# The last head's keys rotated at once on VectorE, and a new table of durations for the attention's list scheduler

## The chip, the core and the metric

The kernel runs on one core of one Trainium2 chip. The metric is the device time of one execution in microseconds (us), as a median of several runs; lower is better. The engines are named as in the profile: PE is TensorE, DVE is VectorE, ACT is ScalarE, POOL is GpSimd, and SP issues most of the DMAs. Each engine works through its own queue in order.

## What is computed

One layer of an encoder on 1024 tokens of width 1024, in float32. Cut to what matters here:

```python
h = x @ w_in
q, k, v, z = split(h)                      # 4 heads of differential attention: 8 q/k maps of 64
q = apply_rope(q, cos, sin) * 64 ** -0.5   # t * cos + rotate_half(t) * sin
k = apply_rope(k, cos, sin)
p = softmax(where(k_chunk <= q_chunk, q @ k.T, -inf))    # block-causal, chunks of 64
a = p[:, :, 0] - lam * p[:, :, 1]          # two maps of a head are subtracted
oa = rms_norm(a @ v, subln_g)
ob = spatial_gating(gelu(z))               # the other half of the width
x = layer_norm(alpha * x + concat(oa, ob) @ w_out)
x = layer_norm(alpha * x + gated_mlp_with_conv(x))
```

## The kernel before

All large products are made of three single-pass matmuls on split operands (`mm3`: high times high, high times low, low times high), so PE has three matmuls for each tile of a product. The kernel is one stream of stages: input projections and the gating half (up to about 187 us of the span), projections of q and k with their rotation (to about 231 us), attention (to about 362 us), output projection and first layer norm (to about 440 us), gated MLP (to about 865 us) and its output projection.

**Rotation.** For head `h`, `sel` 0 (queries) or 1 (keys) and each `half` of 512 tokens, `mm3` fills one PSUM tile `pt`, and `rope_unit` gives a list of steps. `take`: ACT copies `pt` to the SBUF tile `t1`. `rotate`: SP issues four DMAs that write the rows of `t1`, swapped in blocks of 32, to `t2`. `turn`: `t1` times cos (L444, 128x512), and `t2` times sin (L444). `join`: their sum (L447). `high`: ACT makes two 64x512 high parts (L460 and L461 for queries, L463 and L465 for keys; for keys each is also copied to the other partitions by a DMA). `low`: the two 64x512 differences (L475). `turn`, `join` and `low` can run on DVE or POOL. All units run at once on DVE, but for the key units' lows, which go to POOL, and for the two units of the last head's keys. For those two, ACT copies `pt` to a tile `kr` (L502), and the steps are kept in `late`.

**Attention.** Block `n` is one head and 128 queries (`blocks`: 32 in the order of `PAIRS`). Its steps are `scores` (L545, L546, L549 on PE, for both maps), `rowmax` (L558 for more than 512 keys, one for each map; L560 for both maps at once otherwise; DVE, tile `mx`), `expo` (L570 on ACT, tile `p`), `ratio` (L584, L586, DVE, tile `nr`), `combine` (L591, DVE, writes `p`), `transp` (L608, PE), `evac` (L615, ACT or DVE), `attend` (L622, PE) and, for each pair of blocks, a norm (`norm_o` L632, `norm_mul` L656 on POOL or DVE, L674 and others). Three double PSUM tiles (`SCB = 3`) hold scores; a tile comes free when both of its exponentials are done. Beside that run `wo_load` and `wo_lo` (the first half of `w_out`, L777 on ACT, L781 on DVE or POOL), `ob_split` (L788, L789 on POOL, tile `obT`) and `fill` (parts of the output projection on PE that need no attention, added to `xn` at L811).

The order of all these is set while the program is built, by `ListScheduler`: each operation has engines, a duration (`cost`), dependences, a `rank` and resources that it takes or gives (`sc`, `p0`, `t`, `fk` and so on). At each step the operation of lowest rank that could start, by the given durations, is written into the program. What comes out is a fixed order for each engine. The ranks (`RK`, `FW`, `FO` and the others) are constants at the top. The last head's scores wait, in the scheduler, for both late key units (`need`).

Of the kernel before, what the change touches and what calls it, by code (L numbers as in the profile page):

```python
# [23 lines left out]
H = 4  # L24
# [10 lines left out]
SPAN = []  # L35
SCB = 3
WARM = 10
LATE = 151.7
FW = 112.1
FO = 59.8  # L40
FS = 53.1
# [1 line left out]
FA = 754.9  # L43
FT = -0.3
# [94 lines left out]
def hybrid_layer_kernel(  # L139
# [271 lines left out]
    def tslot(name):  # L411
        return qp.tile([P, 512], F32, tag="t", name=nm(name))
# [14 lines left out]
    def rope_unit(h, sel, half, pt):  # L427

        cols = slice(half * 512, (half + 1) * 512)
        t = {}  # L430

        def take():
            t[1] = tslot("t1")
            A.activation(t[1], pt, AF.Copy, scale=1.0 if sel else QSCALE)

        def rotate():

            t.setdefault(1, pt)
            t[2] = tslot("t2")
            for b in range(0, P, 32):  # L440
                nc.sync.dma_start(t[2][b : b + 32], t[1][b ^ 32 : (b ^ 32) + 32])

        def turn(n, eng=V):
            eng.tensor_tensor(t[n], t[n], (cos_s, sin_s)[n - 1][:, cols], op=ALU.mult)  # L444

        def join(n, eng=V):
            eng.tensor_tensor(t[1], t[1], t[2], op=ALU.add)  # L447

        def high():
            r = t[1]  # L450
            if half == 0 and sel == 0:
                stacks.append([None] * 6)
            st = stacks[h]
            names = ((0, "qs0_"), (1, "qs1_")) if sel == 0 else ((2, "kh0_"), (3, "kh1_"), (4, "kl0_"), (5, "kl1_"))
            if st[names[0][0]] is None:
                for n, name in names:
                    st[n] = stack(name)
            q0, q1, k0, k1 = st[:4]
            if sel == 0:
                A.copy(q0[LOW, cols], r[LOW])  # L460
                A.copy(q1[HIGH, cols], r[HIGH])  # L461
            else:
                A.copy(k0[LOW, cols], r[LOW])  # L463
                nc.sync.dma_start(k0[HIGH, cols].bitcast(F32), k0[LOW, cols].bitcast(F32))
                A.copy(k1[HIGH, cols], r[HIGH])  # L465
                nc.sync.dma_start(k1[LOW, cols].bitcast(F32), k1[HIGH, cols].bitcast(F32))

        def low(n, eng=V):
            r = t[1]
            q0, q1, k0, k1, l0, l1 = stacks[h]  # L470
            o, rows, hi = ((q0[HIGH, cols], LOW, q0), (q1[LOW, cols], HIGH, q1)) [n] if sel == 0 else (
                (l0[LOW, cols], LOW, k0), (l1[HIGH, cols], HIGH, k1)
            )[n]
            hi = hi[rows, cols].bitcast(F32)
            eng.tensor_tensor(o, r[rows], hi, op=ALU.subtract)  # L475
            if sel:
                other = (l0[HIGH, cols], l1[LOW, cols])[n]
                nc.sync.dma_start(other.bitcast(F32), o.bitcast(F32))

        def pick(fn, n):  # L480
            return lambda e="DVE": fn(n, V if e == "DVE" else GP)

        both, cost = ["POOL", "DVE"], {"DVE": 0.61, "POOL": 1.23}
        whole = h == H - 1 and sel == 1
        steps = [] if whole else [(["ACT"], 0.63, take)]
        steps += [(["SP"], 2.4, rotate)] + [(both, cost, pick(turn, n)) for n in (1, 2)]
        steps += [(both, cost, pick(join, 0)), (["ACT"], 1.3, high)]
        return steps + [(both, cost, pick(low, n)) for n in range(2)]

    late = []  # L490
    for h in range(H):
        wt = qw0 if h == 0 else [load_qw(h), load_qw(H + h)]
        for sel in range(2):
            for half in range(2):
                cols = slice(half * 512, (half + 1) * 512)
                pt = ps1()
                for k in range(NK):
                    w = wt[sel]
                    mm3(pt, (w[:, 0, k], w[:, 1, k]), tuple(a[:, cols] for a in xt[k]), k == 0, k == NK - 1)
                if h == H - 1 and sel == 1:  # L500
                    kr = tslot("kr")
                    A.copy(kr, pt)  # L502
                    late.append(rope_unit(h, sel, half, kr))
                else:
                    for n, (engines, _, fn) in enumerate(rope_unit(h, sel, half, pt)):
                        fn("POOL" if sel == 1 and n > 5 else "DVE") if len(engines) > 1 else fn()
    release(qpw)


# [162 lines left out]
    def norm_lo(h, i):  # L672
# [3 lines left out]
        )  # L676

    ls_ = ListScheduler(
        {"sc": SCB, "b1": 8 - 2 * SCB, "p0": 4, "p1": 3, "at": 4, "o": 3, "sq": 1, "t": 4, "fx": 0, "fk": 0, "fa": 0, "ys": 0}
    )  # L680
    add = ls_.add
    cmb, evs, avs, lo_end = {}, {}, {}, {}
    freed = [["fx"] * 4 + ["fk"], ["fk"] * 3, ["fk"] * 3, ["fa"] * 3]
    act = lambda c: 0.06 + c * 0.000834
    dve = lambda c: (c + 62) * 0.00104
    late_end = []
    for n, steps in enumerate(late):
        prev = None
        for m, (eng, cost, fn) in enumerate(steps):
            give = ["t"] * 2 + ["fk"] if m == len(steps) - 1 else []  # L690
            prev = add(eng, cost, fn, [prev], LATE + 20 * n, give=give)
        late_end.append(prev)
    for n in range(NB):
        h, qb = blocks[n]
        need = late_end if h == H - 1 else ()
        i, jq = qb // 2, qb % 2
        L, nb, w = dims(qb)
        pe = 2 * max(L, 256) * 0.000418 + 0.06
        rk = n * 10
        ex = []  # L700
        if nb == 1:
            sc = add(
                ["PE"], 2 * pe, lambda n=n: (scores(n, 0), scores(n, 1)), need, rk + RK["sc"], take=["sc"],
                give=freed[h] if n % NT == NT - 1 else [],
            )
            mx = add(["DVE"], dve(2 * L), lambda n=n: (rowmax(n, 0), rowmax(n, 1)), [sc], rk + RK["mx"])
            for j in range(2):
                ex.append(
                    add(
                        ["ACT"], act(L) + 0.18, lambda n=n, j=j: expo(n, j), [mx] + ex, rk + RK["ex"] + 0.1 * j,  # L710
                        take=[f"p{j}"], give=["sc"] if j else [],
                    )
                )
        else:
            for j in range(2):
                give = freed[h] if n % NT == NT - 1 and j == 1 else []
                sc = add(
                    ["PE"], pe, lambda n=n, j=j: scores(n, j), need, rk + RK["sc"] + 0.1 * j, take=["sc"], give=give
                )
                mx = add(["DVE"], dve(L), lambda n=n, j=j: rowmax(n, j), [sc], rk + RK["mx"] + 0.1 * j)  # L720
                ex.append(
                    add(
                        ["ACT"], act(L) + 0.18, lambda n=n, j=j: expo(n, j), [mx] + ex, rk + RK["ex"] + 0.1 * j,
                        take=[f"p{j}"], give=["sc"],
                    )
                )
        ra = add(["DVE"], 0.08, lambda n=n: ratio(n, 0), ex, rk + RK["ra"])
        ra = add(["DVE"], 0.13, lambda n=n: ratio(n, 1), [ra], rk + RK["ra"])
        cmb[n] = add(["DVE"], dve(L), lambda n=n: combine(n), [ra], rk + RK["cb"], give=["p1"])
        nparts = (qb + 4) // 4  # L730
        for part in range(nparts):
            m = min(4, qb + 1 - part * 4)
# [23 lines left out]
            ["ACT", "DVE"], {"ACT": act(256), "DVE": dve(256)}, lambda e, h=h, i=i: norm_o(h, i, e), [prev], rk + RK["no"],  # L756
            take=["o"], give=["b1"],
        )
        sq = add(["ACT"], 0.62, lambda h=h, i=i: norm_ssq(h, i), [no], nr, take=["sq"], give=["sq"])
        ep = add(["DVE"], 0.08, lambda h=h, i=i: norm_eps(h, i), [sq], nr)  # L760
        rs = add(["DVE"], 0.08, lambda h=h, i=i: norm_rs(h, i), [sq, ep], nr)
        pw = add(["POOL"], 0.65, lambda h=h, i=i: norm_pow(h, i), [rs], rk)
# [82 lines left out]
    for t in range(FILL):  # L845
        r = FO + FS * t + FD
        xl = add(["SP"], 2.2, lambda t=t: x_load(t, 0), (), r, take=["t"])
        prev = ob_end[t]
        for e in range(H, 2 * H):
            prev = add(  # L850
                ["PE"], 0.65, lambda t=t, e=e: fill(t, e), [prev, wo_end[e]], r,
                take=[f"b1/sc:f{t}_{H}"] if e == H else [],
            )
        fe = add(["DVE"], dve(512), lambda t=t: fill_add(t), [prev, xl], r, give=[f"b1/sc:f{t}_{H}"])
        if t >= EARLY:
            continue
        prev = fe
        for e in range(H):
            prev = add(
                ["PE"], 0.65, lambda t=t, e=e: fill(t, e), [prev, wo_end[e], lo_end[e, t // 2]], FA + 20 + FT * t,  # L860
                take=[f"b1/sc:f{t}_0"] if e == 0 else [],
            )
        add(
            ["DVE"], 2 * dve(512), lambda t=t: first_half(t, st_f[t]), [prev], FA + 20 + FT * t,
            take=["ys"], give=[f"b1/sc:f{t}_0", "t"],
        )
# [474 lines left out]
```

## Time and profile before

| | us |
|---|---|
| median of 3 runs | 1094.86 |
| the 3 runs | 1091.37 to 1096.70 |
| the profiled execution's own time | 1093.52 |
| its span, from first to last instruction | 1091.5 |
| busy in the span: PE | 1057.8 |
| DVE | 786.7 |
| ACT | 485.1 |
| POOL | 185.7 |

Busy times are sums over the whole span. PE's share of 97% is an average over stages; where PE waits, and for whom, is seen in the stages alone.

### The profile page before, as it was taken

Reading aid. Unit: us, or ns where it says so; the run is one execution under the profiler, and the core shown is the slowest. Engines: PE = TensorE matmul, PEld = TensorE weight load, DVE = VectorE, ACT = ScalarE, POOL = GpSimd, SP = SyncE. Lnnn points to the kernel's source line nnn. Section 1 sums busy time; section 2 is a strip of 40 time slices with the busy share of each in tenths; the row PEclk is TensorE's granted clock in tenths of the full one; section 3 lists DMA queues with packets and bytes.
Section 4 is the critical chain, followed back from the end, with each engine's and each line's share of the span. In section 5 each row is a group of like instructions: output and inputs, shape, how many; then the busy total and the mean of one; then the engine's idle time right before and its main releaser. Section 6 shows DMA issues by size and latency. Waiting matters only on the chain.

```text
span 1091.5 us, 14034 instructions
## 1 busy us (share of the span) xinstructions
PE 1057.8 (97%) x4974; PEld 873.7 (80%) x4974; DVE 786.7 (72%) x1308; ACT 485.1 (44%) x901; POOL 185.7 (17%) x205
## 2 busy tenths in 40 slices
PE   9999999997999999899999999999999999999995
PEld 6888888876787888678888888888888878888874
DVE  5337256769998658997687677768777689954786
ACT  5411124456777335565345434534544364444441
POOL 0024032218643036400000000000000000000045
PEclk9999999999999999899999999999999999999998
DMA  7600224342200511033332232333224982432322
GB/s 252 169 1 11 97 65 126 103 112 59 59 11 26 176 50 49 13 113 111 121 122 72 107 125 74 110 116 126 68 106 174 305 310 89 135 106 87 107 87 97
DMA packets 58262, 115.92 MB, mean 106 GB/s; under 512 B 7760, under 2 KB 8400, under 8 KB 58192
## 3 DMA queue, kind: packets, MB, share of 16 engines
q1 hardware_dynamic: 57616, 112.93, 31.6%
q0 software_dynamic: 576, 2.10, 0.6%
q8 instruction: 39, 0.64, 0.2%
q14 instruction: 31, 0.25, 0.1%
HBM read 82.23 MB, written 24.38 MB: 98 GB/s over the span
## 4 chain that ended last, share of the span: by engine, by line
PE 85%; DVE 7%; issue 3%; POOL 3%; DMA 1%; ACT 1%; SPq 1%; DVEq 0%; POOLq 0%; ACTq 0%
PE ps L221 26%; PE ps L222 26%; PE ps L223 26%; PE ps L622 2%; PE ps L545 1%; PE ps L608 1%; PE ps L546 1%; DVE x L891 1%; POOL kl L475 1%; PE ps L357 1%; DVE p L591 1%; DMA dq<-w_down 0%; PE ps L930 0%; DVE wT L217 0%; DVE t L444 0%
## 5 line engine op out<-in xcount | busy, mean ns | idle before, releaser
L222 PE MATMUL ps<-do,yo 128*128 128x512 f32 x308 | 120.7, 392 | 3.3 <-DVE do L217 3.3
L221 PE MATMUL ps<-do,yo 128*128 128x512 f32 x308 | 120.2, 392 | 2.0 <-ACT do L216 2.0
L223 PE MATMUL ps<-do,yo 128*128 128x512 f32 x308 | 120.5, 391 | 0.0
L217 DVE TENSOR_TENSOR wT<-wq,wT 128x512 fp32r<-128x512 f32 x88 | 63.1, 719 | 34.2 <-ACT wT L216 34.1
L1268 POOL DMA_DIRECT2D g<-ln_g x1 | 0.6, 598 | 475.5 <-DVE do L217 475.5
L216 ACT ACTIVATE wT<-wq 128x512 fp32r<-128x512 f32 x88 | 55.3, 632 | 50.1 <-PE ps L223 43.4
L217 DVE TENSOR_TENSOR yo<-ya,yo 128x512 fp32r<-128x512 f32 x77 | 55.0, 715 | 24.0 <-ACT yo L216 23.8
L222 PEld LDWEIGHTS ps<-do,yo 128*128 128x128 f32 x308 | 58.2, 189 | 16.7 <-DVE do L217 4.6
L216 ACT ACTIVATE yo<-ya 128x512 fp32r<-128x512 f32 x77 | 48.3, 627 | 48.1 <-PE ps L223 46.0
L221 PEld LDWEIGHTS ps<-do,yo 128*128 128x128 f32 x308 | 58.1, 189 | 14.4 <-ACT do L216 2.4
L223 PEld LDWEIGHTS ps<-do,yo 128*128 128x128 f32 x308 | 58.2, 189 | 12.2
L217 DVE TENSOR_TENSOR wB<-wq,wB 128x512 fp32r<-128x512 f32 x66 | 45.9, 697 | 26.8 <-ACT wB L216 22.4
L217 DVE TENSOR_TENSOR do<-dq,do 128x512 fp32r<-128x512 f32 x66 | 47.4, 718 | 21.8 <-ACT do L216 21.8
L972 DVE TENSOR_TENSOR wq<-wq,wq 128x512 f32<-128x512 f32 x88 | 60.7, 691 | 2.9 <-DMA wq<-w_up 0.3
L216 ACT ACTIVATE wB<-wq 128x512 fp32r<-128x512 f32 x66 | 41.1, 630 | 48.4 <-PE ps L223 33.5
L216 ACT ACTIVATE do<-dq 128x512 fp32r<-128x512 f32 x66 | 41.2, 625 | 46.0 <-DVE yo L217 17.4
L1038 DVE SCALAR_TENSOR_TENSOR c<-g,cw,c 128x1023 f32<-128x1023 f32 (+1 forms) x44 | 56.3, 1280 | 6.5 <-ACT c L1036 6.4
L570 ACT ACTIVATE p<-ps,mx 128x512 f32<-128x512 f32 (+7 forms) x64 | 47.1, 742 | 8.7 <-DVE mx L558 5.7
L221 PE MATMUL ps<-xh,qw 128*128 128x512 f32 x128 | 49.9, 390 | 0.0
L222 PE MATMUL ps<-xl,qw 128*128 128x512 f32 x128 | 49.8, 389 | 0.0
L223 PE MATMUL ps<-xh,qw 128*128 128x512 f32 x128 | 49.8, 389 | 0.0
L221 PE MATMUL ps<-zw,xh 128*128 128x512 f32 x128 | 49.8, 389 | 0.0
(236 smaller groups left out, 2935.8 us busy)
## 6 DMA issues: line engine op xcount, KB each, us to landing
ya<-yd SPq DMA_DIRECT2D x77, 256.0 KB, 3.0
wq<-w_gate SPq DMA_DIRECT2D x44, 256.0 KB, 2.8
wq<-w_up SPq DMA_DIRECT2D x44, 256.0 KB, 2.8
yd<-u SPq DMA_DIRECT2D x22, 512.0 KB, 3.1
dq<-w_down SPq DMA_DIRECT2D x44, 256.0 KB, 4.6
zraw<-w_vz SPq DMA_DIRECT2D x23, 256.0 KB, 3.0
yd<-c SPq DMA_DIRECT2D x11, 512.0 KB, 2.6
qraw<-w_qk SPq DMA_DIRECT2D x8, 512.0 KB, 3.7
```

The lines of the kernel that those rows point to most:

```text
L216: A.activation(hi, src, AF.Copy)
L217: (lo_eng or V).tensor_tensor(lo, src, hi.bitcast(F32), op=ALU.subtract)
L221: PE.matmul(po, lhsT=lh, rhs=rh, start=start, stop=False, skip_group_check=onto)
L222: PE.matmul(po, lhsT=lh, rhs=rl, start=False, stop=False, skip_group_check=onto)
L223: PE.matmul(po, lhsT=ll, rhs=rh, start=False, stop=stop, skip_group_check=onto)
L357: PE.matmul(pt[:, c, :], lhsT=vg[t // 2][:, t % 2, g * P : (g + 1) * P], rhs=wsr[:, g, :], start=True, stop=True)
L475: eng.tensor_tensor(o, r[rows], hi, op=ALU.subtract)
L545: PE.matmul(o[:, 0:ww], lhsT=qs[:, qc], rhs=kh[:, kc], start=True, stop=False)
L570: A.activation(p[:, 0:L].rearrange("p (b n) -> p b n", b=nb), sc, AF.Exp, bias=st_mx[n][:, j : j + 1], accum_out=sm[:, j : j + 1],)
L622: PE.matmul(st_o[h, i][:, j * DV : (j + 1) * DV], lhsT=st_at[h, i][kt // 4][:, kt % 4, j], rhs=vr[kt // 2][:, kt % 2, h * DV : (h + 1) * D ...
L972: sub = lambda o, a, b: V.tensor_tensor(q[o], q[a], q[b], op=ALU.subtract)
L1038: V.scalar_tensor_tensor(t[:, n:S], g[:, 0 : S - n], cw[:, f, 2 - n : 3 - n], t[:, n:S], op0=ALU.mult, op1=ALU.add)
```

## The change

The last head's key units are no longer kept: they run like the others, at the end of the rotation loop, and their lows go to DVE too. The list `late`, the rank `LATE` and the wait `need` fall away. The scheduler starts with 8 instead of 4 free slots `t` and 2 instead of 0 free slots `fk`. Its durations are changed: exponentials get 0.12 us more, `combine` 1.2 times as much, the second `ratio` 0.22 instead of 0.13, `norm_ssq` 0.85 instead of 0.62, `fill` 0.68 instead of 0.65, scores and ACT's slope a little more. The ranks stay.

```diff
-LATE = 151.7
...
-        whole = h == H - 1 and sel == 1
-        steps = [] if whole else [(["ACT"], 0.63, take)]
-        steps += [(["SP"], 2.4, rotate)] + [(both, cost, pick(turn, n)) for n in (1, 2)]
+        steps = [(["ACT"], 0.63, take), (["SP"], 2.4, rotate)]
+        steps += [(both, cost, pick(turn, n)) for n in (1, 2)]
         steps += [(both, cost, pick(join, 0)), (["ACT"], 1.3, high)]
         return steps + [(both, cost, pick(low, n)) for n in range(2)]
...
-                if h == H - 1 and sel == 1:
-                    kr = tslot("kr")
-                    A.copy(kr, pt)
-                    late.append(rope_unit(h, sel, half, kr))
-                else:
-                    for n, (engines, _, fn) in enumerate(rope_unit(h, sel, half, pt)):
-                        fn("POOL" if sel == 1 and n > 5 else "DVE") if len(engines) > 1 else fn()
+                for n, (engines, _, fn) in enumerate(rope_unit(h, sel, half, pt)):
+                    fn("POOL" if sel == 1 and n > 5 and h < H - 1 else "DVE") if len(engines) > 1 else fn()
...
-        {"sc": SCB, "b1": 8 - 2 * SCB, "p0": 4, "p1": 3, "at": 4, "o": 3, "sq": 1, "t": 4, "fx": 0, "fk": 0, "fa": 0, "ys": 0}
+        {"sc": SCB, "b1": 8 - 2 * SCB, "p0": 4, "p1": 3, "at": 4, "o": 3, "sq": 1, "t": 8, "fx": 0, "fk": 2, "fa": 0, "ys": 0}
...
-                        ["ACT"], act(L) + 0.18, lambda n=n, j=j: expo(n, j), [mx] + ex, rk + RK["ex"] + 0.1 * j,
+                        ["ACT"], act(L) + 0.3, lambda n=n, j=j: expo(n, j), [mx] + ex, rk + RK["ex"] + 0.1 * j,
...
-        cmb[n] = add(["DVE"], dve(L), lambda n=n: combine(n), [ra], rk + RK["cb"], give=["p1"])
+        cmb[n] = add(["DVE"], both_sb(L), lambda n=n: combine(n), [ra], rk + RK["cb"], give=["p1"])
```

How this moves instructions is seen in the built programs. Rows of the kernel before have its line numbers; in the changed kernel the same lines have numbers 2 smaller in `rope_unit` (L444 is L442), 9 smaller in the attention's steps (L558 is L549, L591 is L582), and 15 smaller behind the scheduler's set-up (L789 is L774).

First DVE at the start of attention. Before, the last query unit's lows (`qs`) are followed by the first row maxima of block 2 (`mx258`, on two score tiles) and the ratios and combines of blocks 0 and 1:

```order
L475 TENSOR_TENSOR qs1_238_1795<-t1240_1825,qs1_238_1795 64x512
L558 TENSOR_REDUCE mx258_1940<-ps2_252_1925 128x1
L584 RECIPROCAL nr262_1952<-sm253_1931 128x1
L584 RECIPROCAL nr263_1954<-sm253_1931 128x1
L558 TENSOR_REDUCE mx258_1940<-ps2_259_1942 128x1
L586 SCALAR_TENSOR_TENSOR nr262_1952<-sm253_1931,nlam_79,nr262_1952 128x1
```

Now the same place, where `t1243` and `t1250` are the two halves of the last head's keys, `kl` their lows, and `mx265` is the maximum of block 2:

```order
L442 TENSOR_TENSOR t1243_1864<-t1243_1864,cos166_1215 128x512
L442 TENSOR_TENSOR t2244_1866<-t2244_1866,sin167_1216 128x512
L549 TENSOR_REDUCE mx265_1982<-ps2_262_1970 128x1
L445 TENSOR_TENSOR t1243_1864<-t1243_1864,t2244_1866 128x512
L442 TENSOR_TENSOR t1250_1911<-t1250_1911,cos166_1215 128x512
L442 TENSOR_TENSOR t2251_1913<-t2251_1913,sin167_1216 128x512
L473 TENSOR_TENSOR kl0_247_1876<-t1243_1864,kh0_245_1874 64x512
L473 TENSOR_TENSOR kl1_248_1877<-t1243_1864,kh1_246_1875 64x512
L445 TENSOR_TENSOR t1250_1911<-t1250_1911,t2251_1913 128x512
L575 RECIPROCAL nr270_1998<-sm260_1967 128x1
L577 SCALAR_TENSOR_TENSOR nr270_1998<-sm260_1967,nlam_79,nr270_1998 128x1
L473 TENSOR_TENSOR kl0_247_1876<-t1250_1911,kh0_245_1874 64x512
```

Ten key operations (one more `kl1` follows the last row shown) now stand around the first maximum of block 2 and ahead of its second one.

Then ACT at the same place. Before, the casts of the last query unit are followed at once by the exponentials of block 0 (`p0_254`, `p1_256`):

```order
L460 CAST qs0_237_1794<-t1240_1825 64x512
L461 CAST qs1_238_1795<-t1240_1825 64x512
L570 ACTIVATE p0_254_1932,sm253_1931<-ps2_248_1907,mx251_1923 128x128
L570 ACTIVATE p1_256_1936,sm253_1931<-ps2_248_1907,mx251_1923 128x128
L570 ACTIVATE p0_257_1938,sm253_1931<-ps2_250_1916,mx255_1934 128x256
```

Now, where `kh` is a key's high part:

```order
L459 CAST qs1_238_1795<-t1240_1825 64x512
L461 CAST kh0_245_1874<-t1243_1864 64x512
L463 CAST kh1_246_1875<-t1243_1864 64x512
L561 ACTIVATE p0_261_1968,sm260_1967<-ps2_254_1943,mx258_1962 128x128
L561 ACTIVATE p1_264_1978,sm260_1967<-ps2_254_1943,mx258_1962 128x128
L561 ACTIVATE p0_267_1986,sm260_1967<-ps2_257_1955,mx263_1976 128x256
L561 ACTIVATE p1_269_1994,sm260_1967<-ps2_257_1955,mx263_1976 128x256
L461 CAST kh0_245_1874<-t1250_1911 64x512
```

The two casts of the first key half moved ahead of the first exponential, and those of the second half between blocks 1 and 2.

Last POOL, behind the lows of the third head's keys. Before, a norm's power and the late key operations (`kr`, and `t2286`, its rotated copy) come first:

```order
L475 TENSOR_TENSOR kl1_226_1697<-t1228_1731,kh1_224_1695 64x512
L651 TENSOR_TENSOR rs284_2022<-rs284_2022,mhalf_75 128x2
L444 TENSOR_TENSOR kr243_1864<-kr243_1864,cos166_1215 128x512
L444 TENSOR_TENSOR t2286_2031<-t2286_2031,sin167_1216 128x512
L444 TENSOR_TENSOR kr245_1891<-kr245_1891,cos166_1215 128x512
```

Now the splits of `obT` do:

```order
L473 TENSOR_TENSOR kl1_226_1697<-t1228_1731,kh1_224_1695 64x512
L773 CAST obT256_1952<-uT52_250 128x128
L774 TENSOR_TENSOR obT256_1952<-uT52_250,obT256_1952 128x128
L773 CAST obT259_1964<-uT52_250 128x128
L774 TENSOR_TENSOR obT259_1964<-uT52_250,obT259_1964 128x128
```

Eight of the 32 pairs of `obT` splits moved ahead of the first norm, and no key operation of the last head is left on POOL. On SP the eight rotating DMAs of the two units moved ahead of two loads of `x` and two of `w_out`. In the whole attention, DVE has 19 instead of 16 evacuations (L615), 4 instead of 7 copies L632 and 7 instead of 9 products L656; the numbers of scores, maxima and combines are the same.

## Rows read from the trace of the kernel before

**Rows 1.** The page's first line.

```profile
span 1091.5 us, 14034 instructions
```

**Rows 2.** Windows by stage: window, its length, then busy (instructions) and PE clock.

```profile
core 0: us, PE busy (x) PEld busy (x) DVE busy (x) ACT busy (x) POOL busy (x), PEclk, DMA share, GB/s
...
230.00:270.00 40.00, 32.85 (x204) 26.92 (x202) 38.37 (x69) 26.29 (x70) 21.65 (x22) 0.91 0.25 74
270.00:290.00 20.00, 17.89 (x117) 14.45 (x117) 18.02 (x35) 14.29 (x43) 13.76 (x27) 1.00 0.27 79
290.00:347.00 57.00, 56.48 (x406) 48.92 (x406) 54.09 (x119) 44.40 (x131) 24.95 (x48) 1.00 0.02 6
347.00:362.00 15.00, 13.34 (x90) 11.43 (x88) 7.60 (x17) 5.42 (x16) 4.41 (x4) 1.00 0.17 54
362.00:440.00 78.00, 78.00 (x376) 65.24 (x375) 54.97 (x108) 31.38 (x77) 32.05 (x29) 1.00 0.30 95
```

**Rows 3.** A window of 4 us behind attention's first stall, same columns.

```profile
236.00:240.00 4.00, 4.00 (x15) 2.64 (x14) 3.80 (x10) 2.45 (x6) 0.00 (x0) 0.57 0.26 66
```

**Rows 4.** Waits of PE from 230 to 362 us: total, times, longest.

```profile
PE ps L608 <- DVE p L591: 2.2, 1, 2.2
```

**Rows 5.** Timeline of DVE from 230 us: start, duration, instruction.

```profile
231.89 0.69 DVE L447 TENSOR_TENSOR t<-t,t 128x512 f32<-128x512 f32 x1
...
233.54 1.40 DVE L475 TENSOR_TENSOR qs<-t,qs 64x512 fp32r<-64x512 f32 x2
234.87 1.08 DVE L558 TENSOR_REDUCE mx<-ps 128x1 f32<-128x896 f32 x1
...
236.12 1.07 DVE L558 TENSOR_REDUCE mx<-ps 128x1 f32<-128x896 f32 x1
```

**Rows 6.** Timeline of ACT, last query cast to the end of block 0's exponentials.

```profile
233.25 0.61 ACT L461 CAST qs<-t 64x512 fp32r<-64x512 f32 x1
...
234.50 0.20 ACT L570 ACTIVATION_READ_ACCUMULATOR p<-ps,mx 128x1 f32 x1
```

**Rows 7.** Timeline of PE at its first wait in attention; idle time in brackets.

```profile
234.75 0.47 PE L545 MATMUL ps<-kh,qs 128*128 128x448 f32 x1 [1.80 <-ACT p L570]
```

**Rows 8.** Timeline of SP's queue, the landing of kr's DMAs, and ACT's first cast of w_out.

```profile
222.90 4.76 SPq L441 DMA_DIRECT2D t<-t  x7
...
232.60 4.95 SPq L441 DMA_DIRECT2D t<-kr  x8
...
DMA to landing us min/median/max: 1.9/2.0/2.3
...
253.36 0.63 ACT L777 ACTIVATE ow<-oraw 128x512 fp32r<-128x512 f32 x1
```

**Rows 9.** Work on kr from 235 to 280 us (DVE, ACT, POOL), and POOL's sine products.

```profile
235.00:280.00 45.00, 1.35 (x2) 2.45 (x4) 9.96 (x6) 0.92 0.26 75
...
L444 POOL TENSOR_TENSOR t<-t,sin 128x512 f32<-128x512 f32 x2 | 2.7, 1367 | 0.0
```

**Rows 10.** Timeline of DVE, instructions that ran beside POOL's late key operations.

```profile
246.48 1.50 DVE L656 TENSOR_TENSOR o<-o,rs 128x256 f32<-128x256 f32 x1
...
249.48 1.53 DVE L591 SCALAR_TENSOR_TENSOR p<-p,nr,p 128x640 f32<-128x640 f32 x1
...
269.83 1.51 DVE L591 SCALAR_TENSOR_TENSOR p<-p,nr,p 128x768 f32<-128x768 f32 x1
...
275.92 1.05 DVE L586 SCALAR_TENSOR_TENSOR nr<-sm,nlam,nr 128x1 f32<-128x1 f32 x1
```

**Rows 11.** The same lines over the run: min/median/max in ns, or busy and mean.

```profile
L656 DVE TENSOR_TENSOR o<-o,rs x9: 416/426/1501, 246.5 to 363.9; 128x256 f32<-128x256 f32 x9
...
L586 DVE SCALAR_TENSOR_TENSOR nr<-sm,nlam,nr x32: 204/220/1137, 237.1 to 349.2; 128x1 f32<-128x1 f32 x32
...
L591 DVE SCALAR_TENSOR_TENSOR p<-p,nr,p 128x512 f32<-128x512 f32 x4 | 3.0, 748 | 0.1
...
L591 DVE SCALAR_TENSOR_TENSOR p<-p,nr,p 128x384 f32<-128x384 f32 x4 | 2.5, 615 | 0.1
...
L615 DVE COPY at<-ps 128x512 f32<-128x512 f32 (+3 forms) x16 | 9.0, 562 | 2.3 <-PE ps L608 2.0
```

More of the change, by code (lines that the diff above doesn't have):

```diff
@@ L436, in rotate @@
         def rotate():
-            t.setdefault(1, pt)
             t[2] = tslot("t2")
@@ L483, in rope_unit @@
         both, cost = ["POOL", "DVE"], {"DVE": 0.61, "POOL": 1.23}
-        whole = h == H - 1 and sel == 1
-        steps = [] if whole else [(["ACT"], 0.63, take)]
-        steps += [(["SP"], 2.4, rotate)] + [(both, cost, pick(turn, n)) for n in (1, 2)]
+        steps = [(["ACT"], 0.63, take), (["SP"], 2.4, rotate)]
+        steps += [(both, cost, pick(turn, n)) for n in (1, 2)]
         steps += [(both, cost, pick(join, 0)), (["ACT"], 1.3, high)]
         return steps + [(both, cost, pick(low, n)) for n in range(2)]
-    late = []
     for h in range(H):
@@ L683, in hybrid_layer_kernel @@
     freed = [["fx"] * 4 + ["fk"], ["fk"] * 3, ["fk"] * 3, ["fa"] * 3]
-    act = lambda c: 0.06 + c * 0.000834
+    act = lambda c: 0.06 + c * 0.00085
+    both_sb = lambda c: 1.2 * dve(c)
     dve = lambda c: (c + 62) * 0.00104
[L686 to L692, printed above, removed]
     for n in range(NB):
         h, qb = blocks[n]
-        need = late_end if h == H - 1 else ()
+        need = ()
         i, jq = qb // 2, qb % 2
         L, nb, w = dims(qb)
-        pe = 2 * max(L, 256) * 0.000418 + 0.06
+        pe = 2 * max(L, 256) * 0.000428 + 0.015 * nb + 0.06
         rk = n * 10
@@ L722, in hybrid_layer_kernel @@
                     add(
-                        ["ACT"], act(L) + 0.18, lambda n=n, j=j: expo(n, j), [mx] + ex, rk + RK["ex"] + 0.1 * j,
+                        ["ACT"], act(L) + 0.3, lambda n=n, j=j: expo(n, j), [mx] + ex, rk + RK["ex"] + 0.1 * j,
                         take=[f"p{j}"], give=["sc"],
@@ L727, in hybrid_layer_kernel @@
         ra = add(["DVE"], 0.08, lambda n=n: ratio(n, 0), ex, rk + RK["ra"])
-        ra = add(["DVE"], 0.13, lambda n=n: ratio(n, 1), [ra], rk + RK["ra"])
-        cmb[n] = add(["DVE"], dve(L), lambda n=n: combine(n), [ra], rk + RK["cb"], give=["p1"])
+        ra = add(["DVE"], 0.22, lambda n=n: ratio(n, 1), [ra], rk + RK["ra"])
+        cmb[n] = add(["DVE"], both_sb(L), lambda n=n: combine(n), [ra], rk + RK["cb"], give=["p1"])
         nparts = (qb + 4) // 4
@@ L758, in hybrid_layer_kernel @@
         )
-        sq = add(["ACT"], 0.62, lambda h=h, i=i: norm_ssq(h, i), [no], nr, take=["sq"], give=["sq"])
+        sq = add(["ACT"], 0.85, lambda h=h, i=i: norm_ssq(h, i), [no], nr, take=["sq"], give=["sq"])
         ep = add(["DVE"], 0.08, lambda h=h, i=i: norm_eps(h, i), [sq], nr)
@@ L850, in hybrid_layer_kernel @@
             prev = add(
-                ["PE"], 0.65, lambda t=t, e=e: fill(t, e), [prev, wo_end[e]], r,
+                ["PE"], 0.68, lambda t=t, e=e: fill(t, e), [prev, wo_end[e]], r,
                 take=[f"b1/sc:f{t}_{H}"] if e == H else [],
@@ L859, in hybrid_layer_kernel @@
             prev = add(
-                ["PE"], 0.65, lambda t=t, e=e: fill(t, e), [prev, wo_end[e], lo_end[e, t // 2]], FA + 20 + FT * t,
+                ["PE"], 0.68, lambda t=t, e=e: fill(t, e), [prev, wo_end[e], lo_end[e, t // 2]], FA + 20 + FT * t,
                 take=[f"b1/sc:f{t}_0"] if e == 0 else [],
```

## The prediction

> **What bounds the kernel now.** The span is 1091.5 us [rows 1], the profiled execution's own time 1093.52 us, so 2.0 us lie around the span. PE is busy for 97% of the span, but that share is an average, so I read the windows by stage first. From 362 to 440 us, behind attention, PE is busy for all 78 us, and no edit there can gain. In attention the picture changes with time [rows 2]. From 230 to 270 us PE is busy for 32.85 of 40 us while DVE is busy for 38.37: DVE sets the pace and PE waits. From 290 to 347 us PE is busy for 56.48 of 57 us and DVE for 54.09: both are nearly full, and what DVE is late by at 290 us, PE has no room to make good. So the place to look is DVE's queue at the start of attention, where the change puts its work.
>
> Second, I read the waits and the timeline there. PE's first wait is 1.80 us and ends at 234.75 us, when ACT's exponentials of block 0 free a score tile [rows 7]. Its longest is 2.2 us, for a combine on DVE [rows 4]. [...]
>
> **What the change costs, part by part.** The sum is made against the profiled execution's 1093.52 us, which is 1.3 us below the median of 1094.86; the runs spread over 5.3 us.
>
> *Key operations to DVE.* Ten operations of the last head's keys run on DVE: for each half two products and one sum of 128x512 and two lows of 64x512. A sum takes 0.69 us and a low half of 1.40, 0.70 us [rows 5]; the products have the size of the sum and are taken as 0.69. That is 6 x 0.69 + 4 x 0.70 = 6.9 us. Before, DVE did two of them, 1.35 us [rows 9]. Added: 5.6 us.
>
> *What stands behind them.* DVE ends the last query lows at 233.54 + 1.40 = 234.94 us [rows 5]. From there the new order has two products (to 236.3), the first maximum of block 2 with 1.08 us (237.4) and the sum (238.1). Only then can ACT make the first two key casts of 0.61 us [rows 6], which stand ahead of the exponentials of block 0: they end at 239.3. Block 0's two exponentials took from 233.86 to 234.70 us, 0.84 us [rows 6], so they end at 240.2 us instead of 234.70. PE's wait of 1.80 us becomes 7.3, 5.5 us more. Meanwhile DVE does two products, two lows, a sum, a ratio (0.3 us) and two lows, to 243.3 us; there the second maximum of block 2 starts, 7.2 us behind its 236.12 [rows 5]. Everything of attention is queued behind it on DVE.
>
> I do not add the 5.5 us of PE to DVE's 5.6: they are the same delay seen from two engines. In the 40 us that follow PE has 7.15 us of idle time [rows 2] because it waits for DVE, so what counts there is DVE's queue. Price of the PE gap by itself: nothing if DVE stays the pacer, 5.5 us if it does not (first rival).
>
> *What is taken off POOL.* The late key operations occupied POOL for 9.96 us on `kr` and 2.7 us on the sine products, 12.7 us in all [rows 9]. Off the path by themselves, but DVE instructions beside them are longer. L656 took 1.50 us at 246.48, against a median of 0.43. L591 of 640 took 1.53; from 0.615 for 384 and 0.748 for 512 columns, 0.133 for 128, 640 would be 0.88. L591 of 768 took 1.51 against 1.01, and L586 1.05 against 0.22 [rows 10, 11]. Excess: 1.07 + 0.65 + 0.50 + 0.83 = 3.1 us, which goes. The bounds are nothing (other POOL work moves up and collides in its place: L781 is still there) and the whole 12.7 us. I take 3.1, which is read from the rows themselves.
>
> [...]
>
> *The scheduler's other choices.* DVE gets three more evacuations at a mean of 0.56 us [rows 11], 1.7 us, three fewer copies L632 and two fewer products L656. Both are 128x256; taking both at L656's median of 0.43, -2.1 us. Net -0.4 us. `obT` splits move to the time in which POOL waited for the first norm; a quarter of them is early, at no price. If that cover were gone they would stand where they stood before.
>
> *DMAs.* The two units issue as many DMAs as before, earlier. SP's seven before them end at 222.90 + 4.76 = 227.66 us; eight took 4.95 us, 0.62 each, and landing takes 2.0 us [rows 8]. The first unit's four land at 227.7 + 2.5 + 2.0 = 232.1 us, before DVE asks for them at 235. The second unit's, even if issued no earlier than 232.60 as before, land at 237.1, before 238.1. So no wait arises. The loads of `x` and `w_out` come 5.0 us later; ACT's first cast of `w_out` is at 253.36 us [rows 8], which hides that. Were this cover gone, at most those 5.0 us would show at `fill`, which is PE's filler and not on the chain.
>
> *The new durations and slots* change no work, only the order. Their price is that of a stall that appears or goes: from -1.66 us (the idle time of PE from 347 to 362 us [rows 2]) to +3.9 (the stall of 2.2 us [rows 4] with a 1.7 us stretch at the low clock behind it). I take 0, between the two: the new table moves no engine's total.
>
> Sum on DVE, the pacer: 5.6 - 0.4 - 3.1 = +2.1 us. Forecast: 1093.5 + 2.1 = 1095.6 us.
>
> **The rivals.** *A: the start gap stays in the time (slower).* PE, not DVE, turns out to be what attention lacks: the 5.5 us it loses at 234 to 240 us are never given back, because from 290 us on PE is full [rows 2]. It decides from the point where DVE, relieved of POOL, has more slack than PE. The gap also brings low clock to work that then matters, one stretch more, 1.7 us. 1093.5 + 5.5 + 1.7 = 1100.7 us. For it: 56.48 of 57 us. Against it: DVE's 38.37 of 40 us before. [...]
>
> *B: the order suffers.* The ranks stand against durations they were not paired with; two more stalls like the 2.2 us one [rows 4], each with its low stretch, cost 2 x 3.9 = 7.8 us: 1093.5 + 2.1 + 7.8 = 1103.4 us. For it: PE's idle times hang on single combines. Against it: work on DVE keeps its amounts, and PE has filler.
>
> *C: much more relief (faster).* All 12.7 us of POOL's late work had held DVE up: 1093.5 + 5.6 - 0.4 - 12.7 = 1086.0 us. For it: four neighbours were longer by up to 1.07 us. Against it: only 3.1 us of excess stand in the rows, and PE's loss at the start alone leaves little room, since PE's idle time from 230 to 362 us is 7.15 + 2.11 + 0.52 + 1.66 = 11.4 us [rows 2].
>
> *D: DVE swallows its extra work* in its own idle time, 1.63 + 1.98 = 3.6 us from 230 to 290 us [rows 2]: 1095.6 - 3.6 = 1092.0. It is counted with the forecast, since both are no change that can be told.
>
> **How the numbers follow.** What can be told from no change is about 0.5%, 5.5 us: below 1089.4 is faster, above 1100.3 slower. Forecast with D 0.65, A 0.15, B 0.12, C 0.08. So faster 0.08, same 0.65, slower 0.27. The range leaves out B and C, 0.20 together: from D less PE's 1.66 us before 362, 1090.3, to A plus the 1.3 us by which the median stood above the profiled run, 1102.0. The predicted time is the forecast's, 1095.6.
>
> **What would show it.** Right: PE's first wait in attention is some 7 us long and ends near 240 us; the first exponential follows two key casts; no DVE instruction beside a key operation on POOL; DVE busy for 95% or more of 235 to 270 us; attention ends, with the last filler run of PE starting solid, about 2 us later than 362. Wrong: a wait of PE below 4 us there; DVE idle for over 3 us from 240 to 270 (then A); new PE waits of over 2 us after 260 us (B); DVE's L591 and L586 at their shortest throughout and attention ending before 358 us (C). If key DMAs landed after DVE asks for them, my account of SP's queue fails too.

## The result, and the profile after

| | us |
|---|---|
| before, median of 6 runs | 1095.26 |
| after, median of 6 runs | 1100.84 (1099.69 to 1102.25) |
| ratio, 95% interval | 1.0051 (1.0039 to 1.0063) |
| profiled execution after, its span | 1102.25, 1100.5 |

The change costs 5.6 us, 0.51%, and the interval excludes no change. That is at the line that the prediction drew between "same" and "slower" (0.5%, 5.5 us), a hair beyond it. It is inside the predicted range, 5.2 us above the predicted time, and within 0.2 us of the number of rival A. Whether A's reason is the right one too was the first question.

The profile after, windows by stage; they answer to [rows 2]:

```profile
230.00:270.00 40.00, 29.75 (x173) 23.66 (x172) 37.81 (x68) 26.99 (x68) 18.51 (x31) 0.83 0.36 109
270.00:290.00 20.00, 19.99 (x143) 17.28 (x143) 15.43 (x36) 14.14 (x46) 4.80 (x10) 1.00 0.05 14
290.00:347.00 57.00, 53.08 (x361) 45.30 (x360) 49.96 (x110) 38.95 (x115) 24.77 (x47) 0.97 0.02 6
347.00:362.00 15.00, 14.55 (x101) 12.43 (x100) 12.23 (x26) 10.40 (x29) 6.71 (x6) 1.00 0.18 54
362.00:440.00 78.00, 77.83 (x384) 64.84 (x383) 50.62 (x101) 28.82 (x70) 29.14 (x25) 1.00 0.29 92
```

Up to 270 us PE is 3.1 us less busy than before. From 270 to 290 us it is full, where it had lost 2.1. Then comes what nobody looked for: from 290 to 347 us, full before (56.48 of 57 us), PE is busy for 53.08 and the clock is 0.97.

The start itself went as predicted. Timeline of ACT, PE and DVE, answering to [rows 5 to 7]:

```profile
237.88 0.62 ACT L461 CAST kh<-t 64x512 fp32r<-64x512 f32 x1 [4.03 <-DVE t L445]
...
239.17 0.37 ACT L561 ACTIVATE p<-ps,mx 128x128 f32<-128x128 f32 x1
...
240.03 0.74 PE L536 MATMUL ps<-kh,qs 128*128 128x448 f32 x1 [7.11 <-ACT p L561]
...
243.72 1.09 DVE L549 TENSOR_REDUCE mx<-ps 128x1 f32<-128x896 f32 x1
```

PE's first wait is 7.11 us, ends at 240.03 (worked out: 7.3 and 240.2), and the second maximum of block 2 starts at 243.72 (worked out: 243.3). The granted clock falls in it, to 0.50 from 236 to 244 us (windows of 4 us; answers to [rows 3]):

```profile
232.00:236.00 4.00, 0.92 (x5) 0.56 (x4) 3.91 (x7) 1.24 (x2) 0.00 (x0) 0.86 0.38 105
236.00:240.00 4.00, 0.00 (x0) 0.00 (x0) 3.97 (x7) 2.07 (x7) 1.34 (x2) 0.50 0.81 268
240.00:244.00 4.00, 3.97 (x11) 2.74 (x12) 3.52 (x7) 3.22 (x8) 3.76 (x8) 0.50 0.72 200
244.00:248.00 4.00, 3.29 (x15) 2.34 (x16) 3.97 (x8) 2.66 (x6) 2.77 (x9) 0.86 0.85 245
```

To see what became of the gap I compare amounts of work. Each matmul record is weighted by its columns and the weights are summed from 170 us on. The lag is the difference of the times at which a kernel and the one before reach the same sum. In us, at six times of the kernel before (the experiments stand below):

```
time before     245    278    296    322    331    414
after           6.3    2.2    0.7    1.8    6.1    5.7
e1_table        0.5   -0.1   -0.9    0.2   -1.1   -2.2
e2_early        6.8    2.9    0.7    0.3   -0.6   -1.8
e3_no           6.2    0.9   -0.7    0.2   -1.2   -2.1
e4_late_dve     2.3   -1.7   -2.9   -1.7   -2.9   -4.0
e5_fd           5.9    2.5    1.3    2.5    0.9    0.1
e6_lows         6.4    2.2    0.7    1.6    0.1   -0.7
e7_pool         8.2    9.3    7.0    7.7    6.5    5.5
e8_ranks        2.6   -0.7   -1.6   -3.5   -4.3   -3.3
e9_gap         -0.9   -1.1   -2.1   -1.0   -2.5   -1.7
```

After the change PE is 6.3 us late at 245 us, 0.7 us at 296 and 1.8 at 322: the gap is given back. Then it loses 4.3 us within nine, and keeps that loss. (Each row is of one execution. The changed kernel, `e3_no` and `e5_fd` have one order of instructions up to about 300 us and stand at 0.7, -0.7 and 1.3 us at 296, so a single lag is good to some 2 us. At 414 us it can stand up to 3 us below what the medians and ratios say. The two profiled spans differ by 9.0 us; 3.3 of these come behind 440 us, where the order is not touched: before's profiled execution lay 1.7 us below its median, after's 1.4 above.)

The place of the second loss, timeline of PE from 325 us, then of ACT and DVE:

```profile
325.60 0.44 PE L653 MATMUL ps<-ident,o 128*128 128x128 f32 x2
327.36 0.66 PE L599 MATMUL ps<-ident,p 128*128 128x128 f32 x4 [1.32 <-DVE oT L665]
328.69 0.44 PE L653 MATMUL ps<-ident,o 128*128 128x128 f32 x2 [0.68 <-ACT at L606]
330.21 0.49 PE L599 MATMUL ps<-ident,p 128*128 128x128 f32 x2 [1.08 <-DVE oT L665]
...
326.32 0.46 ACT L659 ACTIVATE oT<-ps,sg 128x256 fp32r<-128x256 f32 x1
...
328.05 0.59 ACT L606 COPY at<-ps 128x512 f32<-128x512 f32 x1 [1.28 <-PE ps L599]
...
326.83 0.48 DVE L665 SCALAR_TENSOR_TENSOR oT<-ps,sg,oT 128x256 fp32r<-128x256 f32 x1
...
329.67 0.48 DVE L665 SCALAR_TENSOR_TENSOR oT<-ps,sg,oT 128x256 fp32r<-128x256 f32 x1 [1.46 <-ACT oT L659]
```

The order on PE has, one behind the other, a norm's transposes (L653), a block's (L599), a norm's, a block's. Of the two single PSUM tiles (`b1`) one holds a sum of `attend`, so all four need the other in turn, and each waits until ACT and DVE have emptied it (L659 and L665 for a norm, L606 for a block). Nothing else stands between them on PE (ACT's next exponential, which would free a score tile, starts at 331.01 us, behind the last of the four). That makes 1.32 + 0.68 + 1.08 = 3.1 us of idle PE, and then low clock (windows of 4 us), at most (1 - 0.81) x 4 + (1 - 0.76) x 4 = 1.7 us, since PE stood idle in part of the first window:

```profile
328.00:332.00 4.00, 2.24 (x13) 1.99 (x13) 0.69 (x2) 2.32 (x7) 2.58 (x7) 0.81 0.01 4
332.00:336.00 4.00, 4.00 (x24) 3.56 (x23) 2.44 (x6) 2.81 (x11) 0.00 (x0) 0.76 0.00 0
```

The scheduler knew of it. The start times that it gives while it writes the order (its plan, which is no time of the chip) leave PE idle at this place for 1.47, 0.78, 1.08 and 0.52 us, 3.9 in all. So theory 1 for the experiments: the start gap is given back, and what is left is some 1.8 us of key work and one stall of 4.2 that the new order has. Theory 2 is rival A: the gap itself stays in the time. Theory 3: the new table spoils the order, wherever the keys are.

### The profile page after: what moved, and what is told of

Same layout as the page of the kernel before. It is cut to its first block, busy times and chain, and to the rows that moved or that the text cites. A ratio compares the mean times of both kernels' runs of the same rounds, so it can differ in the third digit from the quotient of the medians.

```text
span 1100.5 us, 14044 instructions
## 1 busy us (share of the span) xinstructions
PE 1064.0 (97%) x4974; PEld 877.9 (80%) x4974; DVE 785.7 (71%) x1313; ACT 485.6 (44%) x901; POOL 176.9 (16%) x200
## 4 chain that ended last, share of the span: by engine, by line
PE 53%; DVE 5%; issue 1%; DMA 1%; SPq 0%; ACT 0%; POOL 0%; DVEq 0%
PE ps L221 18%; PE ps L220 18%; PE ps L222 18%; DVE x L876 1%; DMA dq<-w_down 1%; DVE wT L216 0%; DVE S2l L216 0%; DVE yo L216 0%; DVE stt L1236 0%; DVE do L216 0%; DVE A22l L216 0%; SPq L1143 0%; DVE wq L957 0%; DVE x L1212 0%; DVE S4l L216 0%
## 5 line engine op out<-in xcount | busy, mean ns | idle before, releaser
L561 ACT ACTIVATE p<-ps,mx 128x128 f32<-128x128 f32 (+7 forms) x64 | 47.3, 742 | 8.8 <-DVE mx L551 3.9
```

Source lines behind the costliest of these rows:

```text
L561: A.activation(p[:, 0:L].rearrange("p (b n) -> p b n", b=nb), sc, AF.Exp, bias=st_mx[n][:, j : j + 1], accum_out=sm[:, j : j + 1],)
```

## The experiments

Each ratio is taken against the kernel before, run beside it on the same chip. Its median was 1095.3 us beside `e1_table` to `e4_late_dve`, 1094.1 beside `e5_fd` to `e8_ranks`, and 1094.4 beside `e9_gap` and `e4b_late_dve`, so kernels of different groups are compared by their ratios.

**The two halves of the change, one at a time.** `e1_table` is the kernel before with the new durations and late keys:

```diff
-    act = lambda c: 0.06 + c * 0.000834
+    act = lambda c: 0.06 + c * 0.00085
+    both_sb = lambda c: 1.2 * dve(c)
...
-                        ["ACT"], act(L) + 0.18, lambda n=n, j=j: expo(n, j), [mx] + ex, rk + RK["ex"] + 0.1 * j,
+                        ["ACT"], act(L) + 0.3, lambda n=n, j=j: expo(n, j), [mx] + ex, rk + RK["ex"] + 0.1 * j,
...
-        cmb[n] = add(["DVE"], dve(L), lambda n=n: combine(n), [ra], rk + RK["cb"], give=["p1"])
+        cmb[n] = add(["DVE"], both_sb(L), lambda n=n: combine(n), [ra], rk + RK["cb"], give=["p1"])
```

> The kernel before with the new durations alone; the last head's keys stay late. Theory 1 (the start gap is given back, and the 5.6 us are +1.8 us of key work on DVE and +4.2 us of one new stall of PE at 326 to 331 us, which is in the order that the scheduler wrote: its own plan leaves PE idle there for 3.9 us): this kernel has neither the key work on DVE nor, in its plan, an idle time of PE above 0.9 us, so it runs in 1091 to 1097 us, ratio to before 0.996 to 1.002. Theory 2 (the start gap stays in the time): no gap here either, ratio 1.000. Theory 3 (the new durations do not fit the ranks, wherever the keys are): 1.003 to 1.005. So this tells theory 3 from the other two.

Measured: 1095.73 us, 1.0008 (0.9994 to 1.0022). The new durations by themselves cost nothing, and theory 3 falls.

`e2_early` is the changed kernel with the same lines turned back.

> The changed kernel with the old durations: keys rotated at once on DVE, but the table of before. The start gap of PE is the same as in the changed kernel, some 7 us ending near 240 us. Theory 1: the gap is given back by 300 us, the plan holds no chain of idle times as at 326 to 331 us (its longest is 0.8 us), so what stays is DVE's key work: +1.8 us, 1097 us, ratio 1.000 to 1.003. Theory 2: the gap stays, +5.5 to +6.4 us, ratio 1.005 to 1.006.

Measured: 1093.92 us, 0.9987 (0.9976 to 0.9998). The first row is PE's first wait in it, the second that of `e3_no` below:

```profile
239.81 0.74 PE L536 MATMUL ps<-kh,qs 128*128 128x448 f32 x1 [7.04 <-ACT p L561]
```

```profile
239.97 0.74 PE L536 MATMUL ps<-kh,qs 128*128 128x448 f32 x1 [7.08 <-ACT p L561]
```

The same gap as after the change, and no loss: theory 2 falls. It is also below what theory 1 gave (1.000 to 1.003): the 1.8 us of key work do not show. Each half by itself costs next to nothing; only together do they give the order with the stall.

**The stall alone.** `e3_no` lowers one rank of the changed kernel, that of the output copies ahead of the norm; `e5_fd` lowers another by one. Either leaves the start as it is.

```diff
-RK = {..., "av": 22.2, "no": 0.3, "nx": -23.1}
+RK = {..., "av": 22.2, "no": -20.0, "nx": -23.1}
```

> The changed kernel with one rank lowered: the copies of the attention's output ahead of the norm (rank no from 0.3 to -20) are taken earlier. The order of PE stands unchanged up to about 300 us, the start gap with it, and the plan's idle chain of 3.9 us (81 to 86 us into the plan, 326 to 331 us in the trace) is gone. Theory 1: the time falls by the 3.1 us of the three waits to the 4.2 us of lag, to 1096.5 to 1098 us, ratio to before 1.001 to 1.003. Theory 2: the start gap is what costs, so nothing changes: 1100.8 us, 1.005.

```diff
-FD = -32.4
+FD = -33.4
```

> The changed kernel with the rank of the fills lowered by one (FD from -32.4 to -33.4) and nothing else. The order changes only from about 300 us on; the start gap stays; the plan's idle chain of 3.9 us goes (longest idle time behind it 0.6). Theory 1 (one stall, a matter of the order): as with the lowered rank of the norm copies, 3 to 5 us below the changed kernel, 1095.5 to 1098 us, ratio to before 1.000 to 1.002. Rival (the earlier norm copies helped in another way than by that stall): 1100.8 us, 1.005.

Measured: 1095.79 us, 1.0001 (0.9992 to 1.0011), and 1095.91 us, 1.0014 (1.0003 to 1.0025). By the ratios they take 5.5 and 4.1 us off the changed kernel's 5.6. `e3_no` is below the range that theory 1 gave it, so the stall was worth more than the 3.1 to 4.2 us that I gave it. The lags agree: between 322 and 331 us the two kernels gain 1.4 and 1.6 us on the kernel before, where the changed kernel loses 4.3. Window from 322 to 332 us, in the changed kernel and then in `e3_no`:

```profile
322.00:332.00 10.00, 6.92 (x50) 6.00 (x49) 5.72 (x14) 4.20 (x15) 7.19 (x18) 0.92 0.01 2
```

```profile
322.00:332.00 10.00, 10.00 (x77) 9.05 (x76) 9.73 (x28) 7.03 (x25) 6.03 (x14) 1.00 0.01 2
```

PE does 77 matmuls where it did 50, without a wait. A rank moved by one is worth most of what the change cost.

**The start gap alone.** `e4_late_dve` is the changed kernel with the key units copied and rotated at once, but their other steps in the scheduler, on DVE and ACT only.

```diff
+                unit = rope_unit(h, sel, half, pt)
+                if h == H - 1 and sel == 1:
+                    late.append(unit[2:])
+                    unit = unit[:2]
...
+        for m, (eng, cost, fn) in enumerate(steps):
+            give = ["t"] * 2 + ["fk"] if m == len(steps) - 1 else []
+            if len(eng) > 1:
+                eng, cost = ["DVE"], 0.7
+            prev = add(eng, cost, fn, [prev], LATE + 20 * n, give=give)
```

> The changed kernel with the start gap taken away: the last two key units are copied and rotated by DMA at once, but their products, sums, casts and lows are given to the scheduler (rank 110.7 and 130.7), on DVE and ACT alone. DVE does the same work as in the changed kernel, and POOL none of it. PE's first wait falls from 7.1 us back to about 1.8. Theory 1: DVE's work stays, so the time is before's plus 1.8 us, 1097 us, ratio 1.000 to 1.003, give or take stalls in an order that is new from 250 us on (one of 2 us and its low clock are 3.9 us). Theory 2: without the gap the loss is gone, at or below before: ratio 0.997 to 1.000.

Measured: 1092.03 us, 0.9967 (0.9956 to 0.9979). I had PE's first wait wrong: it is 4.53 us, since a key product that waits for its DMA (0.86 us, to 235.36) stands ahead of the first maxima on DVE. And it is faster than theory 1 allowed, by what theory 2 would have it. So the gap was taken out of that kernel: `e9_gap` has the plan hold the key steps back for 5 us (those of the second half for 10, since both holds stand in one queue, `KEYS`), and `e4_late_dve` ran once more beside it, as `e4b_late_dve`.

```diff
-        prev = None
+        prev = add(["KEYS"], 5.0, lambda: None, (), -100)
```

> The kernel with the late key operations on DVE (0.9967 of before), in which PE still waited 4.5 us at the start, since a key product that waits for its DMA stood ahead of the first maxima on DVE. Here the scheduler's plan holds the key operations back for 5 us, so the first maxima stand ahead of them; DVE's work is the same, the plan's idle time of PE about the same (9.8 us for 9.4). PE's first wait falls to about 1.8 us. Theory 1 (what PE loses at the start is given back while DVE works off its queue): within 1 us of the other, ratio 0.996 to 0.998. Theory 2 (the start gap stays in the time): 2.7 us less, 0.994.

> The kernel with the late key operations on DVE once more, beside the one without its start gap, on the same chip: 0.9967 as before (0.9956 to 0.9979), and PE's first wait 4.5 us.

Measured: `e9_gap` 1092.40 us, 0.9975 (0.9964 to 0.9986); `e4b_late_dve` 1090.95 us, 0.9965 (0.9954 to 0.9977). PE's first wait in `e4b_late_dve`, then in `e9_gap`:

```profile
237.27 0.54 PE L542 MATMUL ps<-kh,qs 128*128 128x448 f32 x1 [4.53 <-ACT p L567]
```

```profile
234.77 0.74 PE L542 MATMUL ps<-kh,qs 128*128 128x448 f32 x1 [1.79 <-ACT p L567]
```

2.7 us less gap, and not faster. In the lags the lead of some 3 us at 245 is gone at 278. This is no clean second test of theory 2, though. In `e9_gap` DVE's instructions beside POOL's are about 3 us longer in sum than in `e4_late_dve` (the amounts stand at the end of the next section), which may have eaten the 2.7 us. What theory 2 falls by is `e2_early` and `e3_no`, which have the whole gap and no loss.

**DVE's key work.** `e6_lows` is `e3_no` with the last head's four lows on POOL (`and h < H - 1` left out).

> The kernel with the lowered rank of the norm copies (which ran at 1.0001 of before), and the last head's four lows on POOL like those of the other heads. DVE loses 2.8 us of work in 238 to 243 us; the orders of PE and SP stay. Theory 1 (DVE is the pacer at the start of attention): -2.8 us, less up to 1 us for DVE instructions beside POOL's lows: 1093 to 1094.5 us, ratio 0.997 to 0.999. Rival 1 (the 7.1 us wait of PE, which this leaves, sets the time): 1.000. Rival 2 (what DVE gains it loses again beside POOL, whose lows also delay the obT splits behind them): 1.000 to 1.002.

Measured: 1095.74 us, 1.0013 (1.0003 to 1.0023), where `e3_no` had 1095.79. No gain: theory 1 is wrong here, and the time is where rivals 1 and 2 put it. The waits of DVE from 234 to 300 us show why:

```profile
DVE mx L549 <- PE ps L540: 3.0, 3, 1.1
```

In `e3_no` no such wait stands there (in the changed kernel and in `e5_fd`, with the same order at this place, one of 1.2 and one of 1.1 us). Most of the 2.8 us that DVE no longer works, it waits for PE's scores: behind the gap the chain from exponentials through a score tile to scores to a maximum is about as long as DVE's queue. Rival 2 has a share in it, as DVE's instructions beside POOL's lows are longer (one L577 takes 0.92 us at 245.53, against 0.26 in `e3_no`); the two are not told apart. Cutting DVE's queue alone gains nothing.

**POOL beside DVE.** `e7_pool` adds eight products of 128x512 on POOL to `e3_no`, on data that nobody reads, each behind a combine:

```diff
+    dum = ap.tile([P, 512], F32, name="dum")
+    prev = add(["POOL"], 0.0, lambda: GP.memset(dum, 0.0), (), -100)
+    for n in range(8):
+        prev = add(["POOL"], 0.0, lambda: GP.tensor_tensor(dum, dum, dum, op=ALU.mult), [prev, cmb[n]], -100)
```

> The kernel with the lowered rank of the norm copies (1.0001 of before), and eight added products of 128x512 on POOL alone, one behind each of the first eight combines, on data that nobody reads; the scheduler's plan does not see them, so all other orders stay. At 1.37 us each they are 11 us of POOL, where the late key operations before were 12.7. My term for DVE's relief from those was 3.1 us; the traces of before and after show 4.7 us less excess on DVE from 231 to 300 us. Theory 1 (a DVE instruction beside a product on POOL is about 0.4 us longer, and DVE is the pacer): +2.7 to +4.1 us, ratio 1.0025 to 1.004. Rival (no such price): 1.000. Rival C (DVE is held up for all of POOL's time): +11 us, 1.010.

Measured: 1101.50 us, 1.0070 (1.0053 to 1.0087), 7.6 us above `e3_no` by the ratios (5.7 by the medians, of two chips): more than theory 1 gave, less than rival C. The products took 1.16 us each, 9.3 in all. Of the costliest groups of DVE from 231 to 300 us, in `e7_pool` and then in `e3_no`:

```profile
L577 DVE SCALAR_TENSOR_TENSOR nr<-sm,nlam,nr 128x1 f32<-128x1 f32 x15 | 6.1, 405 | 0.2
...
L549 DVE TENSOR_REDUCE mx<-ps 128x1 f32<-128x768 f32 x4 | 3.8, 945 | 0.0
...
L582 DVE SCALAR_TENSOR_TENSOR p<-p,nr,p 128x640 f32<-128x640 f32 x2 | 2.7, 1364 | 0.0
...
L582 DVE SCALAR_TENSOR_TENSOR p<-p,nr,p 128x512 f32<-128x512 f32 x2 | 1.8, 920 | 0.0
```

```profile
L577 DVE SCALAR_TENSOR_TENSOR nr<-sm,nlam,nr 128x1 f32<-128x1 f32 x18 | 4.0, 221 | 0.2
...
L549 DVE TENSOR_REDUCE mx<-ps 128x1 f32<-128x768 f32 x4 | 3.8, 946 | 0.0
...
L582 DVE SCALAR_TENSOR_TENSOR p<-p,nr,p 128x640 f32<-128x640 f32 x2 | 1.8, 880 | 0.0
...
L582 DVE SCALAR_TENSOR_TENSOR p<-p,nr,p 128x512 f32<-128x512 f32 x2 | 1.5, 738 | 0.0
```

The ratios' second step (L577, 405 ns for 221) and these combines (L582, 1364 for 880 and 920 for 738) are longer, and they read SBUF alone; these maxima (L549, 945 for 946), which read PSUM, are not. `e3_no` has such an instruction too (a combine of 768 at 259.10 took 1.70 us), so the sum over all forms counts. Taking for each form of DVE instruction its lower quartile over all these traces as undisturbed, the excess from 231 to 300 us is 8.1 us in `e7_pool` and 3.5 in `e3_no`: 4.6 us, 0.6 for each product. The longest new wait of PE is the same excess, seen from PE: 3.0 us at 275.21, where `e3_no` has 0.17 at this point of the order. PE waits for a norm's L665 on DVE, behind two ratios and two combines that took 2.7 us more than in `e3_no` (the last of them 1.85 us for 0.89):

```profile
272.04 1.85 DVE L582 SCALAR_TENSOR_TENSOR p<-p,nr,p 128x640 f32<-128x640 f32 x1
...
275.21 0.67 PE L599 MATMUL ps<-ident,p 128*128 128x128 f32 x3 [2.99 <-DVE oT L665]
```

```profile
267.08 0.89 DVE L582 SCALAR_TENSOR_TENSOR p<-p,nr,p 128x640 f32<-128x640 f32 x1
...
269.28 0.55 PE L599 MATMUL ps<-ident,p 128*128 128x128 f32 x3 [0.17 <-DVE oT L665]
```

POOL's own queue adds to that, with `w_out` parts and norm steps that stand behind added products: PE waits 1.3 us for a part of `w_out` (L770) and 0.4 us for a norm (L647).

```profile
PE ps L221 <- POOL ow L770: 1.3, 1, 1.3
...
PE ps L653 <- POOL o L647: 0.4, 1, 0.4
```

With the 4.6 us these make 6.3, an estimate that takes them as additive, of the 5.7 to 7.6 measured.

**Other ranks.** `e8_ranks` is `e4_late_dve` with all ranks (`RK`, `FW`, `FO`, `FS`, `FD`, `FA`, `FT`, `LATE`) searched for little idle time of PE in the plan.

> The kernel with the late key operations on DVE in the scheduler (0.9967 of before) with other ranks, searched so that the plan, with the new durations, leaves PE idle for less time: 6.6 us instead of 9.4. Theory 1 (idle time in the plan is idle time on the chip): 2.8 us less, 1089 us, ratio 0.994. Rival (the plan's durations are too far from the chip's for its idle times to count beyond chains of several us): 0.997, or slower.

Measured: 1092.13 us, 0.9981 (0.9969 to 0.9993), where `e4_late_dve` had 1092.03. The rival holds: 2.8 us less of scattered idle time in the plan, none over 1.1 us long in either, gain nothing. In this kernel the plan is a guide to long chains only.

The fastest version is `e4_late_dve`: 0.9967 and 0.9965 of before, some 9 us below the changed kernel. Against before that is 0.3%, clear of 1 by its interval, but below the 0.5% that the prediction would call a change.

## Why the prediction was right, and where it was off

**The range.** That 1100.84 us lies in the range is in good part luck. The range reached up to 1102.0 us for rival A alone (1100.7 + 1.3), and A's mechanism is not what happened; a stall that the new order makes was rival B's, which the range left out.

**The start.** Right. The gap had the size, the end and the cause worked out, and it adds nothing to the time, as I took it: `e2_early` and `e3_no` have it and lose nothing. Of the signs, DVE is busy for 32.97 of 35 us from 235 to 270, 94% where 95 were asked for, and idle for 2.0 us from 240 to 270, where A asked for 3. That DVE is the pacer was too simple, though: in the first microseconds it and PE are links of one chain (`e6_lows`), and only behind that does DVE's queue decide.

**Key operations, relief, redistribution.** The lags of the changed kernel, 0.7 us at 296 and 1.8 at 322, are near the +2.1 forecast. But the runs with all three parts and no stall are not that much slower: `e2_early` is 1.4 us faster than before (0.9976 to 0.9998) and `e3_no` even with it (0.9992 to 1.0011). So no whole run shows a cost of 2.1 us. One term was mis-sized, the relief: I took -3.1 us from four rows. By the excess over the lower quartiles DVE loses 8.0 us beside POOL from 231 to 300 us before and 3.3 after, so it is -4.7, and 5.6 - 0.4 - 4.7 = +0.5, which `e3_no` bears out and which is above `e2_early`; why that one is faster still is open. The rows that answer to [rows 11] agree: L577 at most 0.667 us, where L586 had reached 1.137, and L647 at most 0.505, where L656 had reached 1.501.

```profile
L577 DVE SCALAR_TENSOR_TENSOR nr<-sm,nlam,nr x32: 202/219/667, 241.4 to 355.0; 128x1 f32<-128x1 f32 x32
...
L647 DVE TENSOR_TENSOR o<-o,rs x7: 414/426/505, 293.7 to 372.7; 128x256 f32<-128x256 f32 x7
```

`e7_pool` shows that price from the other side, 0.6 us of excess for each product of 1.16 us, half of what rival C would have.

**The new durations and slots: the step that failed.** "I take 0, between the two: the new table moves no engine's total." No work was added, and the term came out at +4.3 us in the lags and at 4.1 to 5.5 us by what `e5_fd` and `e3_no` take off, beyond its upper bound of 3.9. It was there to be read: four groups of transposes that need one PSUM tile in turn, with nothing between them on PE. I looked at the order at the start, where instructions had moved by design, and gave the rest a number. Rival B had the mechanism and the unit (2.2 us of wait, 1.7 of low clock), but asked for two such stalls, and for single waits of over 2 us as the sign; here three shorter ones stand in a row. The 1.7 us, in B as in A and in the upper bound, is (1 - 0.57) x 4 from [rows 3]; behind the wait of 2.2 us itself the kernel before has a clock of 0.58 from 260 to 264 us, which gives the same.

**Rival A** gave 1100.7 us and 1100.84 were measured, for a reason that is not the one: its loss is given back, and another of about the same size comes 90 us later. That the two numbers meet is chance. Only the lags and the experiments tell the two apart.

What stays open: why `e4_late_dve` is faster than `e2_early` and `e3_no`. That DVE's excess there is the smallest (2.7 us from 231 to 300) speaks for the key operations kept off POOL without a queue of them at the start; `e9_gap`, with 5.7 us of excess, is as fast within 1.5 us, so it isn't shown.

## What to carry to other kernels

When a table of durations changes in a list scheduler, the total work of no engine moves, but the order does everywhere, and one chain of operations that share the last buffer can cost more than the edit that was meant: look through the whole new order, or the scheduler's own plan, for a run of instructions on the bottleneck engine that all need the same buffer with nothing between them. A gap at the start of a stage can cost nothing where another engine's queue sets the pace behind it (here 7.04 and 7.08 us of it, at 0.9987 and 1.0001 of before); compare the amounts of work done at several times, since two losses of one size at different places look the same in the total. And try a neighbouring rank before a change is thrown out.

## What the runs showed of the hardware

In `e3_no` POOL instructions were longer too beside DVE's: the casts of `obT` (128x128) that ran beside DVE's key operations took up to 0.75 us, where most others of the same kind took 0.29. And in the changed kernel the granted clock, at 0.50 from 236 to 244 us, was back to 1.00 for the whole of 250 to 260 us; with the gap given back by 296 us, those microseconds at 0.50 did not stay in the time.
